# Sums of squares of the queries in a sliding-window attention layer: from small products on TensorE to transposes and sums on VectorE

## The chip, the cores and the metric

The kernel runs on one core of one Trainium2 chip. The metric is the device time of one execution in microseconds (us). Three runs of the kernel before took 1942.86, 1943.02 and 1943.11 us, so the median is 1943.02 us.

## The reference, cut to what matters

The reference is a decoder trunk of two layers on 1024 tokens of width 1024, in float32. Layer 0 mixes tokens by a short gated convolution, layer 1 by attention, and each is followed by a SwiGLU channel mixer. The change lies in the attention layer. There each of the 16 query heads of 64 features is normalised by its own root mean square before the scores are taken:

```python
def rmsnorm(x, gain):
    r = lax.rsqrt(jnp.mean(x * x, axis=-1, keepdims=True) + EPS)
    return (x * r) * gain

q = qkv[..., :q_end].reshape(bsz, s, N_KV_HEADS, GROUP, HEAD_DIM)
q = rmsnorm(q, q_gain)           # k in the same way
scores = einsum('bnqkgd,bnskd->bnkgqs', qb, kw) * scale   # blocks of 128 queries, 256 keys
logits = concatenate([scores - slope * dist (masked), sink], -1)
p = softmax(logits)[..., :-1]
out = einsum('bnkgqs,bnskd->bnqkgd', p, vw) @ w_o
```

So for each token and each query head one number is needed: the sum of the squares of 64 features.

## The kernel before, in words

Activations lie with features on the 128 partitions and tokens along the free axis. Every float32 product is made of three products in a reduced float32 format: each operand is split into a high and a low part (`hi`, `lo`), and hi*hi, hi*lo and lo*hi are added in PSUM. The large matrix products of the channel mixers are cut by a seven-product scheme; none of that is touched.

In the attention layer the 16 query heads are 8 tiles of 128 features (two heads each), numbered `i`. `project_k`, `project_v` and the tile-0 projection come first. Then, from line 1952, everything on TensorE, ScalarE, VectorE and GpSimd is in an order written out by hand. The loop at line 1965 projects tile `i` (the generator `product`, lines 165 and 169) in eight steps of six matmuls of 512 columns; `step` (line 1873) interleaves each of these steps with one unit of attention, a unit being one query tile and one block of 128 tokens. Units run ten steps behind the projection. The letters of `ORDER = "SPTMEDkPHLVOPK"` give the order inside a step:

- S: scores of the unit on TensorE (lines 1725 and 1726) into the one buffer of PSUM bank P0. M: VectorE adds the distance bias and takes the maximum, reading P0 (line 1739). E: exponentials of the unit before, on ScalarE (line 1757).
- T: the exponentials of two units before are transposed on TensorE (line 1765) into bank P1 or P3. H and L: ScalarE and VectorE split them into high and low parts (lines 1772 and 1778). V: product with the values, of three units before (lines 1790 and 1791). O: ScalarE and VectorE keep the result (lines 1807 and 1808).
- P, three times: two projection matmuls each. D: division steps that fall due; they use GpSimd (line 1596), four transposes (line 1601) and VectorE (line 1835).
- k and K: what has been planned with `plan(d, f)`. A `d` of x.5 runs at the k of the step after x, a whole `d` at the K that ends step x, counting from 0 at the first step after the tile's projection.

`keep_q(i, acc)` (line 1636) plans the rest of a projected query tile. `acc` is a pair of PSUM banks out of four, which the tile after next will use again. ScalarE squares both halves (`squares`, line 1654) from PSUM into `side`. `stats_of` (line 1656) makes eight products on TensorE: a block of 128 squared features x 128 tokens is the stationary operand and a matrix of two columns of ones and zeros, `half`, the moving one, so each token gets two sums (line 1513). VectorE scales them and adds epsilon (`head_mean`, line 1520), ScalarE takes Ln and Exp (lines 1532 and 1537), VectorE refines (lines 1539 to 1546). ScalarE copies the projected tile to `raw` in the slot G7 (line 1644). GpSimd spreads the factors to 64 columns each (`wide_of`, line 1596), TensorE turns them back to the feature layout (`rows_of`, line 1601) and VectorE multiplies `raw` (line 1606). `part_hi` (ScalarE, line 1681) and `part_lo` (GpSimd, line 1687) split the result into the operands of the scores. After each of the steps 0, 2, 3 and 5 a quarter of the next weights is split on ScalarE (line 137) and GpSimd (line 140).

Each engine runs its instructions in the order written, so an instruction that waits holds up those behind it.

Of the kernel before, what the change touches and what calls it, by code (L numbers as in the profile page):

```python
# [13 lines left out]
ALU = mybir.AluOpType  # L14

P = 128
D = 1024
T = 1024
NK = D // P
NB = T // P  # L20
# [61 lines left out]
def trunk_kernel(ctx: ExitStack, tc: tile.TileContext, xT, small, w_in, w_out, w_qk, w_v, w_o, w_gu, w_dn, out):  # L82
# [3 lines left out]
    dve, act, pool, pe = nc.vector, nc.scalar, nc.gpsimd, nc.tensor  # L86
    uid = [0]

    def slot(tag, shape=(P, D), dtype=F32, bufs=1):
        uid[0] += 1  # L90
        return sb.tile(list(shape), dtype, tag=tag, name=f"{tag}_{uid[0]}", bufs=bufs)
# [4 lines left out]
    def bank(tag):  # L96
        uid[0] += 1
        return pm.tile([P, 512], F32, tag=tag, name=f"{tag}_{uid[0]}", bufs=4 if tag == "acc" else 1)

    def plain(ap):  # L100
        return ap.bitcast(F32)
# [681 lines left out]
    def sums_of(a11, a12, a21, a22, s2, s3, s1, s4):  # L783

        return [
            lambda: dve.tensor_tensor(s3, a11, a21, ALU.subtract),
            lambda: dve.tensor_tensor(s2, a22, s3, ALU.subtract),  # L787
            lambda: dve.tensor_tensor(s4, a12, s2, ALU.subtract),
            lambda: dve.tensor_tensor(s1, a21, a22, ALU.add),
        ]  # L790
# [707 lines left out]
    def attention_layer():  # L1498
# [11 lines left out]
        def head_stats(st, sq, b0, n):  # L1510
            for b in range(n):
                o = 2 * (b0 + b)
                pe.matmul(st[:, o : o + 2], sq[:, b * P : (b + 1) * P], half, start=True, stop=True)
# [1 line left out]

        def head_mean(st):
            m = slot("hr_m", (P, NB, 2), bufs=2)
            dve.scalar_tensor_tensor(  # L1520
                m,
                st[:, 0 : 2 * NB].rearrange("p (b h) -> p b h", h=2),
                1.0 / HD,
                eps_r.unsqueeze(2).to_broadcast([P, NB, 2]),
                ALU.mult,
                ALU.add,
            )
            return m

        def head_log(m):  # L1530
            y = slot("hr_y", (P, NB, 2), bufs=3)
            act.activation(y, m, AF.Ln)
            return y

        def head_guess(y, inv):

            act.activation(y, y, AF.Exp, scale=-0.5)
            t = slot("hr_t", (P, NB, 2), bufs=2)
            dve.tensor_tensor(t, y, y, ALU.mult)
            if inv is not None:  # L1540
                dve.tensor_tensor(y, y, inv.unsqueeze(1).to_broadcast([P, NB, 2]), ALU.mult)
            return t

        def head_newton(y, t, m):
            dve.scalar_tensor_tensor(t, t, -0.5, m, ALU.mult, ALU.mult)
            dve.scalar_tensor_tensor(y, t, 1.5, y, ALU.add, ALU.mult)

        def head_r(m):
            y = head_log(m)
            head_newton(y, head_guess(y, None), m)  # L1550
            return y
# [41 lines left out]
        def spread(eng, wide, y):  # L1593

            copy = act.copy if eng is act else eng.tensor_copy
            copy(wide.rearrange("p (b h d) -> p b h d", b=4, h=2), y.unsqueeze(3).to_broadcast([P, 4, 2, HD]))

        def turn_blocks(pb, wide):
            for b in range(4):
                t = slice(b * P, (b + 1) * P)  # L1600
                pe.transpose(pb[:, t], wide[:, t], ident)  # L1601

        def scale_rows(raw, wide, q, pb):
            turn_blocks(pb, wide)
            c = slice(q * 512, q * 512 + 512)
            dve.tensor_tensor(raw[:, c], raw[:, c], pb, ALU.mult)

        def keep_k(g, raw, y):
# [13 lines left out]
                dve.tensor_tensor(lo[rest, e, :], raw[rows, :], plain(hi[rows, e, :]), ALU.subtract)  # L1622
            kz[g] = (hi, lo)

        g2 = slot("G2")
        s_bufs = [slot("s0", (P, 2, 2 * P))]
        s_bufs += [g2[:, h * 512 : h * 512 + 512].rearrange("p (e c) -> p e c", e=2) for h in (0, 1)]
# [8 lines left out]
        def keep_q(i, acc):  # L1636

            t = {}

            def copy(h):  # L1640
                if h == 0:
                    t["raw"] = slot("G7") if i + 1 < NK else t["both"][:, 0, :]
                src, c = acc.parts[h]
                act.copy(t["raw"][:, c], src)

            def squares(h):
                if h == 0:
                    if i + 1 < NK:
                        side = slot(f"G{5 + i % 2}")
                    else:  # L1650
                        t["both"] = slot("XS5", (P, 2, D))
                        side = t["both"][:, 1, :]
                    t["side"] = [side[:, h * 512 : h * 512 + 512] for h in (0, 1)]
                act.activation(t["side"][h], acc.half(h), AF.Square)

            def stats_of():
                t["st"] = bank(pos["free"])
                for h in (0, 1):
                    head_stats(t["st"], t["side"][h], 4 * h, 4)

            def mean():
                t["m"] = head_mean(t["st"])
                t["y"] = head_log(t["m"])

            def guess():
                t["t"] = head_guess(t["y"], cst[:, C_INVS + 2 * i : C_INVS + 2 * i + 2])

            def newton():
                head_newton(t["y"], t["t"], t["m"])


            def halves(e):
                rows = [slice(0, HD), slice(HD, P)]
                return rows[e], rows[1 - e]

            def part_hi(h, e):
                rows, _ = halves(e)
                if h == 0 and e == 0:
                    Q[i] = [slot(f"G{3 + i % 2}", dtype=F32R), slot(f"G{5 + i % 2}", dtype=F32R)]
                c = slice(h * 512, h * 512 + 512)  # L1680
                act.copy(Q[i][e][rows, c], t["raw"][rows, c])

            def part_lo(h, e):
                rows, rest = halves(e)
                c = slice(h * 512, h * 512 + 512)
                q = Q[i][e]
                pool.tensor_tensor(q[rest, c], t["raw"][rows, c], plain(q)[rows, c], ALU.subtract)

            rows_of = lambda h: scale_rows(t["raw"], t["side"][h], h, bank(pos["free"]))
            wide_of = lambda h: spread(pool, t["side"][h], t["y"][:, 4 * h : 4 * h + 4, :])  # L1690

            first, rows = (1, (4.5, 5.5)) if i + 1 < NK else (0, (5.5, 6.5))
            for d, fs in (
                (first, [lambda: squares(0)]),
                (first + 0.5, [lambda: squares(1)]),
                (1.5 + first, [stats_of, mean]),
                (2 + first, [guess, newton]),
                (rows[0] - 1.5 if first else 0, [lambda: copy(0)]),
                (rows[0] - 1.5, [lambda: wide_of(0)]),
                (rows[0] - 0.5 if first else 1, [lambda: copy(1)]),  # L1700
                (rows[0] - 0.5, [lambda: wide_of(1)]),
                (rows[0], [lambda: rows_of(0)]),
                (rows[1], [lambda: rows_of(1)]),
                (rows[1], [lambda: part_hi(0, 0), lambda: part_hi(0, 1)]),
                (rows[1] + 0.5, [lambda: part_lo(0, 0)]),
                (rows[1] + 1, [lambda: part_lo(0, 1)]),
                (rows[1] + 1.5, [lambda: part_hi(1, 0), lambda: part_hi(1, 1), lambda: part_lo(1, 0)]),
                (rows[1] + 2.5, [lambda: part_lo(1, 1)]),
            ):
                for f in fs:  # L1710
                    plan(d, f)
# [145 lines left out]
        pos = {"n": -LAG, "step": 0, "free": "P1"}  # L1857
        agenda = {}

        def plan(d, f):  # L1860

            agenda.setdefault(pos["step"] + d, []).append(f)
# [55 lines left out]
        for q in range(2):  # L1918
            raw = slot("WR", bufs=2)
# [10 lines left out]
        k1 = project_k(1)  # L1930
        st = bank("acc")
        head_stats(st, k0[1], 0, NB)
        m0 = head_mean(st)
        y0 = head_r(m0)
        v_ps = project_v(0)
        keep_v(0, v_ps)
        keep_k(0, k0[0], y0)
        st = bank("acc")
        head_stats(st, k1[1], 0, NB)
        m1 = head_mean(st)  # L1940
        y1 = head_r(m1)
        v_ps = project_v(1)
        keep_v(1, v_ps)
# [2 lines left out]
        acc = Acc()  # L1946
# [4 lines left out]
        E = mybir.EngineType  # L1951
        with tc.manual_schedule(engines={E.PE, E.Activation, E.DVE, E.Pool}):
            keep_q(0, acc)
            w = load_w(w_qk[1], NK, dve, pool)

# [9 lines left out]
            for i in range(1, NK):  # L1965
                acc = Acc()
                work = product(acc, w, xs)
                for k in range(NK):
# [10 lines left out]
                    if k in (0, 2, 3, 5):  # L1979
                        j = 2 * (0, 2, 3, 5).index(k)  # L1980
# [7 lines left out]
            free = ["XS3", "XS4"]  # L1988
            first_w = {}
            for m in range(NK):  # L1990
                acc = Acc()
                work = product(acc, w, o_split, len(early))
                for k in range(len(early)):
# [5 lines left out]
                    if m == NK - 1 and k == 0:  # L1999
# [4 lines left out]
                        for t, tag in enumerate(("WH", "WL")):  # L2004
                            raw = slot("WR", (P, len(late) * P), bufs=2)
# [16 lines left out]
        for e in (0, 1):  # L2022
            wide, rows, scale = divisions[NK // 2 - 1, 1, e]
# [22 lines left out]

    conv_layer()
    attention_layer()


# [87 lines left out]
```

## Time and profile before

| | |
|---|---|
| Median of three runs | 1943.02 us |
| Profiled execution | 1943.28 us, of which the span is 1941.4 us |
| TensorE (PE) busy | 1935.1 us (100% of the span) |
| Weight load (PEld) busy | 1618.2 us (83%) |
| VectorE (DVE) busy | 1371.3 us (71%) |
| ScalarE (ACT) busy | 871.2 us (45%) |
| GpSimd (POOL) busy | 246.2 us (13%) |
| DMA | 311.79 MB, mean 161 GB/s |

Busy shares are means over the whole span. The query tiles are projected between about 1025 and 1205 us, and there the shares differ from these means, so they are read from the stretch itself. A matmul on TensorE overlaps the one before it, so its listed duration is longer than the time by which it delays the next one; the time that a group takes on TensorE is the distance between starts, which the chain of waits shows.

### The profile page before, as it was taken

Reading aid. Unit: us, or ns where it says so; the run is one execution under the profiler, and the core shown is the slowest. Engines: PE = TensorE matmul, PEld = TensorE weight load, DVE = VectorE, ACT = ScalarE, POOL = GpSimd, SP = SyncE. Lnnn points to the kernel's source line nnn. Section 1 sums busy time; section 2 is a strip of 40 time slices with the busy share of each in tenths; the row PEclk is TensorE's granted clock in tenths of the full one; section 3 lists DMA queues with packets and bytes.
Section 4 is the critical chain, followed back from the end, with each engine's and each line's share of the span. In section 5 each row is a group of like instructions: output and inputs, shape, how many; then the busy total and the mean of one; then the engine's idle time right before and its main releaser. Section 6 shows DMA issues by size and latency. Waiting matters only on the chain.

```text
span 1941.4 us, 25504 instructions
## 1 busy us (share of the span) xinstructions
PE 1935.1 (100%) x9153; PEld 1618.2 (83%) x9153; DVE 1371.3 (71%) x2432; ACT 871.2 (45%) x1702; POOL 246.2 (13%) x344
## 2 busy tenths in 40 slices
PE   9999999999999999999999999999999999999999
PEld 8888888888888888888898888888888888888887
DVE  8998767876777676765644777788677766775543
ACT  5543434523333335444435888656233333344441
POOL 0000011011111110000004445310111111110000
PEclk9999999999999999999999999999999999999999
DMA  8422185244555548976300000152455455487562
GB/s 318 165 98 87 65 299 189 83 157 175 182 203 179 171 162 286 328 266 205 114 23 23 23 12 18 37 192 61 162 195 181 173 199 179 133 282 275 194 231 100
DMA packets 143167, 311.79 MB, mean 161 GB/s; under 512 B 13888, under 2 KB 53952, under 8 KB 143040
## 3 DMA queue, kind: packets, MB, share of 16 engines
q1 hardware_dynamic: 118992, 225.71, 34.6%
q0 software_dynamic: 23904, 84.42, 11.9%
q8 instruction: 72, 1.18, 0.3%
q14 instruction: 55, 0.45, 0.1%
q10 hardware_dynamic: 144, 0.03, 0.0%
HBM read 219.40 MB, written 90.70 MB: 160 GB/s over the span
## 4 chain that ended last, share of the span: by engine, by line
PE 95%; DVE 2%; issue 1%; ACT 1%; DMA 0%; ACTq 0%; DVEq 0%
PE acc L904 15%; PE acc L905 15%; PE acc L907 15%; PE P L904 9%; PE P L905 9%; PE P L907 9%; PE acc L165 6%; PE acc L169 3%; PE acc L1034 2%; PE acc L1032 2%; PE acc L1033 2%; PE P L1765 1%; PE P L1601 1%; PE P L1725 1%; PE P L1726 1%
## 5 line engine op out<-in xcount | busy, mean ns | idle before, releaser
L904 PE MATMUL acc<-XS,G 128*128 128x512 f32 x894 | 348.2, 389 | 0.0
L907 PE MATMUL acc<-XS,G 128*128 128x512 f32 x894 | 347.8, 389 | 0.0
L905 PE MATMUL acc<-XS,G 128*128 128x512 f32 x894 | 347.8, 389 | 0.0
L907 PEld LDWEIGHTS acc<-XS,G 128*128 128x128 f32 x894 | 167.8, 188 | 34.9
L904 PEld LDWEIGHTS acc<-XS,G 128*128 128x128 f32 x894 | 167.8, 188 | 34.9
L905 PEld LDWEIGHTS acc<-XS,G 128*128 128x128 f32 x894 | 167.8, 188 | 34.7
L907 PE MATMUL P<-A,G 128*128 128x512 f32 x502 | 195.3, 389 | 0.0
L905 PE MATMUL P<-A,G 128*128 128x512 f32 x502 | 195.3, 389 | 0.0
L904 PE MATMUL P<-A,G 128*128 128x512 f32 x502 | 195.3, 389 | 0.0
L907 PE MATMUL acc<-A,G 128*128 128x512 f32 x410 | 159.5, 389 | 0.0
L904 PE MATMUL acc<-A,G 128*128 128x512 f32 x410 | 159.5, 389 | 0.0
L905 PE MATMUL acc<-A,G 128*128 128x512 f32 x410 | 159.5, 389 | 0.0
L844 DVE TENSOR_TENSOR G<-WL,G 128x512 fp32r<-128x512 f32 x168 | 114.9, 685 | 53.1 <-ACT G L843 53.1
L843 ACT CAST G<-WR 128x512 fp32r<-128x512 f32 (+1 forms) x198 | 119.7, 605 | 67.3 <-PE acc L907 29.3
L165 PE MATMUL acc<-XS,WH 128*128 128x512 f32 x480 | 146.3, 405 | 0.6 <-ACT WH L137 0.6
L844 DVE TENSOR_TENSOR G<-WR,G 128x512 fp32r<-128x512 f32 (+1 forms) x198 | 131.8, 666 | 10.8 <-ACT G L843 10.5
L843 ACT CAST G<-WH 128x512 fp32r<-128x512 f32 (+1 forms) x156 | 93.7, 601 | 82.2 <-PE acc L907 36.8
L1204 ACT ACTIVATE G<-G 128x512 f32<-128x512 f32 x88 | 55.8, 634 | 162.1 <-DVE G L1275 158.0
L843 ACT CAST G<-WL 128x512 fp32r<-128x512 f32 x168 | 103.5, 616 | 37.3 <-DVE WL L787 33.5
L904 PE MATMUL P<-XS,G 128*128 128x512 f32 x290 | 112.9, 389 | 0.1
L907 PE MATMUL P<-XS,G 128*128 128x512 f32 x290 | 112.8, 389 | 0.0
L905 PE MATMUL P<-XS,G 128*128 128x512 f32 x290 | 112.8, 389 | 0.0
(316 smaller groups left out, 3898.1 us busy)
## 6 DMA issues: line engine op xcount, KB each, us to landing
G<-h SPq DMA_DIRECT2D x70, 512.0 KB, 5.2
h<-X POOLq DMA_DIRECT2D x44, 512.0 KB, 5.5
X<-in_w_dn SPq DMA_DIRECT2D x80, 256.0 KB, 3.7
s<-X POOLq DMA_DIRECT2D x40, 512.0 KB, 4.7
WR<-in_w_gu SPq DMA_DIRECT2D x36, 512.0 KB, 6.0
WH<-in_w_gu SPq DMA_DIRECT2D x36, 512.0 KB, 6.4
h<-X POOLq DMA_DIRECT2D x66, 256.0 KB, 4.0
WR<-s SPq DMA_DIRECT2D x52, 256.0 KB, 3.4
```

The lines of the kernel that those rows point to most:

```text
L165: pe.matmul(ps.half(h), wh, xs[:, j, c], start=first and j == 0, stop=False)
L169: pe.matmul(ps.half(h), wl, xs[:, 0, c], start=False, stop=last)
L843: lambda: act.copy(out_hi, raw),
L844: lambda: lo_eng.tensor_tensor(out_lo, raw, plain(out_hi), ALU.subtract),
L904: pe.matmul(ps, w[:, 0, c], x[:, 0, :], start=start and e == 0, stop=False, skip_group_check=True)
L905: pe.matmul(ps, w[:, 0, c], x[:, 1, :], start=False, stop=False, skip_group_check=True)
L907: pe.matmul(ps, w[:, 1, c], x[:, 0, :], start=False, stop=last, skip_group_check=True)
L1032: pe.matmul(ps, hi[:, kc], xs[:, 0, c], start=k == 0, stop=False, skip_group_check=True)
L1033: pe.matmul(ps, hi[:, kc], xs[:, 1, c], start=False, stop=False, skip_group_check=True)
L1034: pe.matmul(ps, lo[:, kc], xs[:, 0, c], start=False, stop=k == n_op - 1, skip_group_check=True)
L1204: state["silu"] = act.activation(x, x, AF.Silu)
L1601: pe.transpose(pb[:, t], wide[:, t], ident)
```

## The change

`stats_of` goes, and with it the eight small products of each query tile. The copy of the projected tile to `raw` comes first, both halves of it in the steps 1 (steps 0 and 1 for the last tile). Then `turn_raw(h)` turns four 128x128 blocks of `raw` on TensorE into the half of the accumulator that has just been copied, which puts tokens on the partitions, and ScalarE squares that half into `side`. `sums_of(h)` adds the 64 squares of each head on VectorE (`tensor_reduce`, 512 columns to 8), into the tile that `head_mean` then scales in place. `raw` is one tile in G7 for all query tiles but the last, where before a new one was taken for each. `rows_of`, `part_hi` and `part_lo` are planned one step later, save for the last tile. For the keys nothing changes but how `head_mean` is given its output.

```diff
+        raw_q = slot("G7")
             def copy(h):
                 if h == 0:
-                    t["raw"] = slot("G7") if i + 1 < NK else t["both"][:, 0, :]
+                    t["raw"], t["side"] = raw_q, None
+                    if i + 1 == NK:
+                        both = slot("XS5", (P, 2, D))
+                        t["raw"], t["side"] = both[:, 0, :], both[:, 1, :]
                 src, c = acc.parts[h]
                 act.copy(t["raw"][:, c], src)
-            def squares(h):
+            def turn_raw(h):
...
+                turn_blocks(acc.half(h), t["raw"][:, h * 512 : h * 512 + 512])
                 act.activation(t["side"][h], acc.half(h), AF.Square)
-            def stats_of():
-                t["st"] = bank(pos["free"])
-                for h in (0, 1):
-                    head_stats(t["st"], t["side"][h], 4 * h, 4)
+            def sums_of(h):
+                dve.tensor_reduce(
+                    t["m"][:, 4 * h : 4 * h + 4, :],
+                    t["side"][h].rearrange("p (b h d) -> p b h d", b=4, h=2),
+                    mybir.AxisListType.X,
+                    ALU.add,
+                )
-            first, rows = (1, (4.5, 5.5)) if i + 1 < NK else (0, (5.5, 6.5))
+            d0, rows = 0.5 if i + 1 < NK else 0, (5.5, 6.5)
             for d, fs in (
-                (first, [lambda: squares(0)]),
-                (first + 0.5, [lambda: squares(1)]),
-                (1.5 + first, [stats_of, mean]),
-                (2 + first, [guess, newton]),
-                (rows[0] - 1.5 if first else 0, [lambda: copy(0)]),
+                (d0, [lambda: copy(0)]),
+                (d0 + 0.5, [lambda: copy(1)]),
+                (d0 + 1, [lambda: turn_raw(0)]),
+                (d0 + 1.5, [lambda: sums_of(0)]),
+                (d0 + 2, [lambda: turn_raw(1)]),
+                (d0 + 2.5, [lambda: sums_of(1), mean]),
+                (d0 + 3, [guess, newton]),
                 (rows[0] - 1.5, [lambda: wide_of(0)]),
-                (rows[0] - 0.5 if first else 1, [lambda: copy(1)]),
                 (rows[0] - 0.5, [lambda: wide_of(1)]),
                 (rows[0], [lambda: rows_of(0)]),
                 (rows[1], [lambda: rows_of(1)]),
                 (rows[1], [lambda: part_hi(0, 0), lambda: part_hi(0, 1)]),
                 (rows[1] + 0.5, [lambda: part_lo(0, 0)]),
                 (rows[1] + 1, [lambda: part_lo(0, 1)]),
                 (rows[1] + 1.5, [lambda: part_hi(1, 0), lambda: part_hi(1, 1), lambda: part_lo(1, 0)]),
                 (rows[1] + 2.5, [lambda: part_lo(1, 1)]),
```

## Rows read from the trace of the kernel before

**Rows 1.** The page: busy time of TensorE; shares of the chain that ended last.

```profile
PE 1935.1 (100%) x9153; PEld 1618.2 (83%) x9153; DVE 1371.3 (71%) x2432; ACT 871.2 (45%) x1702; POOL 246.2 (13%) x344
PE 95%; DVE 2%; issue 1%; ACT 1%; DMA 0%; ACTq 0%; DVEq 0%
```

**Rows 2.** Windows in the query tiles: PE, PEld, DVE, ACT, POOL busy, clock, DMA.

```profile
1090.00:1112.00 22.00, 22.00 (x153) 19.96 (x152) 17.40 (x49) 17.75 (x54) 10.50 (x14) 1.00 0.08 26
1156.00:1178.00 22.00, 22.00 (x151) 19.79 (x150) 17.03 (x52) 19.01 (x57) 13.68 (x14) 1.00 0.06 21
```

**Rows 3.** Waits of TensorE's weight loads, 1020 to 1215 us: total, times, longest.

```profile
PEld P L1725 <- DVE mx L1739: 1.4, 6, 0.3
PEld P L1790 <- DVE A L1808: 0.7, 2, 0.5
```

**Rows 4.** Chain of waits around one group of small products: start, length, what.

```profile
1092.72 0.44 PE P L1765 x4
1093.15 1.68 PE P L1513 x16
1094.84 0.57 PE acc L165 x2
```

**Rows 5.** Chain of waits around four transposes of line 1601.

```profile
1034.54 0.44 PE P L1601 x4
1034.97 0.47 PE acc L165 x2
```

**Rows 6.** Line 1513 on TensorE for the query tiles: count, duration min/median/max, first and last start.

```profile
L1513 PE MATMUL P<-cst,G x112: 165/251/251, 1029.8 to 1171.1; 128*128 128x2 f32 x112
L1513 PE MATMUL P<-cst,XS x16: 166/251/251, 1190.8 to 1192.4; 128*128 128x2 f32 x16
```

**Rows 7.** Line 1601 on TensorE for keys and queries, in the same columns.

```profile
L1601 PE MATMUL P<-cst,G x72: 270/272/273, 999.3 to 1180.0; 128*128 128x128 f32 x72
L1601 PE MATMUL P<-cst,XS x8: 271/272/302, 1203.1 to 1206.2; 128*128 128x128 f32 x8
```

**Rows 8.** ScalarE's squares and copies of query tiles, in the same columns.

```profile
L1654 ACT ACTIVATE G<-acc x14: 578/588/597, 1025.4 to 1166.9; 128x512 f32<-128x512 f32 x14
L1644 ACT COPY G<-acc x14: 567/576/591, 1032.3 to 1175.3; 128x512 f32<-128x512 f32 x14
```

**Rows 9.** Groups on VectorE, 810 to 1120 us: busy, mean ns | idle before.

```profile
L139 DVE CAST WH<-WR 128x1024 fp32r<-128x1024 f32 x2 | 1.4, 693 | 14.0 <-PE acc L165 14.0
L1391 DVE TENSOR_TENSOR s<-s,WL 128x512 f32<-128x512 f32 x12 | 8.2, 686 | 0.6 <-ACT WL L1383 0.5
```

**Rows 10.** Groups on GpSimd in the same stretch.

```profile
L1687 POOL TENSOR_TENSOR G<-G,G 64x512 fp32r<-64x512 f32 x16 | 20.6, 1288 | 7.0 <-ACT G L1681 6.2
L140 POOL TENSOR_TENSOR WL<-WR,WH 128x256 fp32r<-128x256 f32 x18 | 13.2, 738 | 56.2 <-ACT WH L137 55.8 <-POOL G L1687 0.2
```

**Rows 11.** Timeline of GpSimd at step 0 of tile 3.

```profile
1085.10 0.61 POOL L1596 COPY s<-den 128x512 f32<-128x512 f32 x1 [0.26 <-DVE den L1825]
```

**Rows 12.** Timeline of TensorE: first scores of steps 2, 3 and 4 of tile 3.

```profile
1088.39 0.28 PE L1725 MATMUL P<-A,G 128*128 128x256 f32 x1
...
1091.61 0.28 PE L1725 MATMUL P<-A,G 128*128 128x256 f32 x1
...
1096.17 0.28 PE L1725 MATMUL P<-A,G 128*128 128x256 f32 x1
```

**Rows 13.** Timeline of ScalarE in step 2 of tile 3: an exponential, a high part.

```profile
1089.01 0.50 ACT L1757 ACTIVATE s<-s,mx 128x256 f32<-128x256 f32 x1
...
1090.47 0.58 ACT L1772 CAST G<-P 128x512 fp32r<-128x512 f32 x1
```

**Rows 14.** Timeline of VectorE in steps 2 and 3 of tile 3: L, O and M.

```profile
1091.08 0.69 DVE L1778 TENSOR_TENSOR G<-P,G 128x512 fp32r<-128x512 f32 x1
1091.81 0.43 DVE L1808 TENSOR_TENSOR G<-P,G 64x256 f32<-64x256 f32 x1
1092.29 0.54 DVE L1739 CUSTOM_DVE_ANT_0 G<-P,cst 128x256 f32<-128x256 f32 x1
```

More of the change, by code (lines that the diff above doesn't have):

```diff
@@ L1513, in head_stats, with head_mean @@
                 pe.matmul(st[:, o : o + 2], sq[:, b * P : (b + 1) * P], half, start=True, stop=True)
-        def head_mean(st):
-            m = slot("hr_m", (P, NB, 2), bufs=2)
+        def head_mean(m, st):
             dve.scalar_tensor_tensor(
                 m,
-                st[:, 0 : 2 * NB].rearrange("p (b h) -> p b h", h=2),
+                st,
                 1.0 / HD,
@@ L1527, in head_mean @@
             )
-            return m
         def head_log(m):
@@ L1641, in copy @@
                 if h == 0:
-                    t["raw"] = slot("G7") if i + 1 < NK else t["both"][:, 0, :]
+                    t["raw"], t["side"] = raw_q, None
+                    if i + 1 == NK:
+                        both = slot("XS5", (P, 2, D))
+                        t["raw"], t["side"] = both[:, 0, :], both[:, 1, :]
                 src, c = acc.parts[h]
                 act.copy(t["raw"][:, c], src)
-            def squares(h):
+            def turn_raw(h):
                 if h == 0:
[L1648 to L1653, printed above, removed]
-                act.activation(t["side"][h], acc.half(h), AF.Square)
-            def stats_of():
-                t["st"] = bank(pos["free"])
-                for h in (0, 1):
-                    head_stats(t["st"], t["side"][h], 4 * h, 4)
+                    side = slot(f"G{5 + i % 2}") if t["side"] is None else t["side"]
+                    t["side"] = [side[:, j * 512 : j * 512 + 512] for j in (0, 1)]
+                    t["m"] = slot("hr_m", (P, NB, 2), bufs=2)
+                turn_blocks(acc.half(h), t["raw"][:, h * 512 : h * 512 + 512])
+                act.activation(t["side"][h], acc.half(h), AF.Square)
+            def sums_of(h):
[5 more added lines that the diff above has]
+                )
             def mean():
-                t["m"] = head_mean(t["st"])
+                head_mean(t["m"], t["m"])
                 t["y"] = head_log(t["m"])
@@ L1932, in attention_layer @@
         head_stats(st, k0[1], 0, NB)
-        m0 = head_mean(st)
+        m0 = slot("hr_m", (P, NB, 2), bufs=2)
+        head_mean(m0, st[:, 0 : 2 * NB].rearrange("p (b h) -> p b h", h=2))
         y0 = head_r(m0)
@@ L1939, in attention_layer @@
         head_stats(st, k1[1], 0, NB)
-        m1 = head_mean(st)
+        m1 = slot("hr_m", (P, NB, 2), bufs=2)
+        head_mean(m1, st[:, 0 : 2 * NB].rearrange("p (b h) -> p b h", h=2))
         y1 = head_r(m1)
```

## The prediction

> **What bounds the kernel now.** I read the page first. TensorE is busy for the whole span and holds 95% of the chain that ended last; no other engine has over 2% of it [rows 1]. So an instruction taken from TensorE's queue shortens the run by its own time, as long as nothing else becomes late. Then the windows, to see whether that also holds where the change is. It does: in the query tiles TensorE fills its 22 us at a granted clock of 1.00, which is its upper level, 2.4 GHz. But the others are far busier there than their means: VectorE 17.0 to 17.4 of 22 us, ScalarE 17.8 to 19.0, GpSimd 10.5 to 13.7 [rows 2]. ScalarE at 81 to 86% is the engine with least room. Then the waits of TensorE's weight loads: between 1020 and 1215 us they are a few tenths each, the largest group 1.4 us in six waits for the maxima, which free the one bank P0 [rows 3]. TensorE is fed, with little to spare. Last come the chain and the timelines, for the price of each group and for the distance between the engines.
>
> **What leaves TensorE.** Eight small products per tile are 16 records, since each product of two float32 operands shows as two: 112 + 16 = 128 in eight tiles [rows 6]. In the chain a group takes 1.68 us, and the pair of projection matmuls behind it 0.57 us [rows 4] where such a pair otherwise takes 0.47 [rows 5]. So one tile pays 1.68 + 0.10 = 1.78 us, eight tiles 14.24 us. All of it is on the path that sets the end.
>
> **What comes to TensorE.** Eight transposes per tile in two groups of four. Line 1601 does the same operation, on blocks of the same size and type, and each of its transposes is one record: the two key tiles and eight query tiles have 80 [rows 7], which is 10 times 8. Four take 0.44 us, and the pair behind them 0.47, so nothing is added behind [rows 5]. Eight cost 0.88 us a tile, 7.04 us in all. The new ones write into an accumulator bank in place of a P bank, which no row shows. If they needed two records each, they would cost what the small products did, 14.24 us, and the gain would be zero. If the bank made no difference, 7.04. I take 7.04, since the transposes of lines 1765 and 1601, into two kinds of use of P banks, take the same 0.44 [rows 4, 5]. Nothing suggests less than that. TensorE's balance is 7.04 - 14.24 = -7.20 us.
>
> **What comes to VectorE.** Sixteen sums of 512 columns. No row shows this operation. From below, a cast of 1024 columns takes 0.693 us, so half of it 0.35; from above, a two-input operation of 512 takes 0.686 [rows 9]. That is 5.6 to 11.0 us in all, 0.7 to 1.4 a tile, in a tile of some 24 us (1029.8 to 1171.1 us is six tiles [rows 6]). I take 0.6, nearer the row of 512, because that has the same number of columns to read. VectorE goes from 79% to some 84% of the stretch, and the sum itself lies beside TensorE's work. Its cost is only in what it holds up.
>
> The Trainium skill speaks against this step: VectorE: DVE Perf Modes, section "Rules for kernel authors", calls this reduction the slowest operation of the engine, always at one element a cycle, and advises to restructure around it. By that page's clock 512 columns are an estimated 0.53 us before overhead. The trace has no such instruction to agree or differ. At the cast's 0.35 the scores of the six tiles that lose anything below would come some 0.25 us earlier each, 1.5 us in all, and the time would be 1936.2; by the rule's 0.53 it is within half a microsecond of my sum.
>
> **What only moves.** ScalarE has the same squares and copies as before, 0.588 and 0.576 us each [rows 8], GpSimd the same splits. Their order and their waits change, and here lie the losses. No DMA is issued by a moved step, and the weight splits on ScalarE and GpSimd keep their places behind steps 0, 2, 3 and 5, with two steps to the next tile.
> - `copy(1)` runs at the end of step 1, right behind the last `part_lo` of the tile before, which has moved to the same place and reads the half of `raw` that the copy overwrites. ScalarE waits there for GpSimd. Queued behind it are the exponentials, the first square and the next high part; the values and transposes on TensorE need those.
> - The first square waits for `turn_raw(0)`, in front of the high part. The transposes it waits for stand right behind those the high part needs anyway: 0.44 us, plus the square.
> - `sums_of` waits for the square, and on VectorE stands in front of the maxima of the next step; scores two steps on wait for these.
> - `turn_raw(h)` waits for a copy that was issued a step or more earlier.
>
> **Tile 3, worked through**, in before's times, each step by its row. On GpSimd a division ends at 1085.10 + 0.61 = 1085.7 [rows 11]. Three `part_lo` of 1.29 and one weight split of 0.74 follow [rows 10]: 1085.7 + 3.87 + 0.74 = 1090.3. ScalarE, by adding its durations, is there at about 1089.8, so it waits 0.5 us. Then copy to 1090.9, two exponentials of 0.5 to 1091.9, square to 1092.5, high part 0.58 to 1093.05 [rows 8, 13]. VectorE: low part 0.69 to 1093.75, keeping 0.43 to 1094.2, sum 0.35 to 0.69 to 1094.55 or 1094.9, two maxima, of which P0 is needed some 1.0 us, to 1095.6 or 1095.9 [rows 9, 14]. TensorE begins step 3 at 1091.61 + 0.44 = 1092.05; that step took 4.56 us with the stats and takes 4.56 - 1.78 + 0.44 = 3.22 now, so the scores of step 4 are due at 1095.27 [rows 4, 5, 12]. They wait 0.3 to 0.6 us; I take 0.5. The second sum and the mean in step 3 come with the same slack and I count nothing more for them.
>
> In an even tile the division falls differently: GpSimd is later, by 1.05 us at the copy, but step 2 has 0.44 us more on TensorE and the first unit's exponentials are short. By the same addition the scores come 0 to 0.2 us late; I take 0.2. So: tiles 3 and 5, 0.5 each; tiles 2, 4 and 6, 0.2 each; tile 7, whose copy needs no G7 and so doesn't wait, 0.3 for its shorter distance from turn to square; tiles 0 and 1 nothing, since few or no units run then. Together 1.0 + 0.6 + 0.3 = 1.9 us. The cover is thin: where a tile has ScalarE late by another 0.5 us, nearly all of it arrives at TensorE.
>
> **The sum.** -14.24 + 7.04 + 1.9 = -5.3 us. The profiled execution took 1943.28 us, span 1941.4 and 1.9 around it, and the median of the runs is 1943.02, 0.26 less. 1943.28 - 5.3 = 1938.0 for a profiled one, and 1937.7 for the median.
>
> **The rivals.**
> - *Nothing waits.* If ScalarE reaches the copy later than GpSimd is done, and the maxima are in time, the whole 7.2 us stays: 1935.8. For it: my chain is late by half a microsecond at most. Against: the waits for the maxima exist already [rows 3] and the new order adds work in front of them.
> - *The queues eat it.* The squares, the copies and the two halves of `part_hi` now stand in five successive steps on an engine at 81 to 86%. If each of tiles 2 to 7 loses 0.55 to 1.2 us in place of my 0.3, 3.3 to 7.2 us are gone: 1939.1 to 1943.0. The same result follows if the transposes take two records: -0 + 1.9, 1944.9.
> - *Slower, by GpSimd in front of the copy.* In tiles 1 to 6 ScalarE stands at `copy(1)` until the last `part_lo` ends. If GpSimd is one `part_lo` and one weight split later than I added, 1.29 + 0.74 = 2.03 us [rows 10], and nothing absorbs it, six tiles lose 12.2 us: 1943.02 - 7.2 + 12.2 = 1948.0. It decides from 1.2 us a tile on (7.2 / 6). For it: in an even tile I find 1.05 us of wait already. Against: exponentials have about a microsecond before their transposes need them, and steps 4 to 6 have less on ScalarE than before, so a delay doesn't grow from tile to tile.
>
> **How the numbers follow.** What a measurement of this kernel can tell from no change is about 0.2%, 3.9 us, so faster means under 1939.1 and slower over 1946.9. The forecast, losses of 1 to 3.3 us, 1936.7 to 1939.1: 0.38. Nothing waits, 1934.8 to 1936.7 (its low end gives back 1 us of today's waits): 0.26. The queues eat it, 1939.1 to 1946.9, the two-record case included: 0.23. Slower through GpSimd, over 1946.9: 0.13. Faster is the first two, 0.64. The range from 1934.8 to 1943.6 leaves out the slower case and some 0.05 of the one before; it holds both ends of the sum's cost and all of the losses up to 7.8 us.
>
> **What would show it.** Line 1513 keeps only the keys' 32 records; 64 more transposes of line 1601 stand in the accumulator banks, 0.44 us a group in the chain. The sums appear on VectorE with 0.35 to 0.69 us. ScalarE shows waits at line 1644 for GpSimd's line 1687, of half a microsecond in odd tiles and one in even ones. TensorE's waits for the maxima, line 1725, grow by one to two microseconds in total. I am wrong if the transposes into the accumulator cost more than 0.44 a group, if line 1725 or 1765 waits over 3 us more, or if TensorE's waits don't grow at all and the gain is whole.

## The result: slower by 0.4%, and the profile after

The changed kernel takes 1951.22 us (median of six runs, 1950.13 to 1953.12) against 1943.01 for the kernel before. The ratio is 1.0043, 95% interval 1.003 to 1.0056. The profiled execution has a span of 1949.5 us, 8.1 more than before. The forecast was 1937.7 and faster; the range ended at 1943.6.

The page of the changed kernel, busy time of TensorE, answers to [rows 1]: its busy time has hardly moved, although it has 64 records fewer.

```profile
PE 1936.0 (99%) x9089; PEld 1611.1 (83%) x9089; DVE 1382.4 (71%) x2448; ACT 870.5 (45%) x1702; POOL 246.6 (13%) x344
```

The instructions are those that were foreseen. Line 1513 (count, duration min/median/max, first and last start) is left with the keys' 32 records, 64 transposes write accumulators, against [rows 6, 7], and the sum on VectorE takes 0.686 us:

```profile
L1513 PE MATMUL acc<-cst,G x32: 165/251/251, 986.2 to 1002.0; 128*128 128x2 f32 x32
L1599 PE MATMUL acc<-cst,G x56: 270/272/273, 1028.7 to 1176.9; 128*128 128x128 f32 x56
L1599 PE MATMUL acc<-cst,XS x8: 270/272/273, 1197.4 to 1199.6; 128*128 128x128 f32 x8
L1658 DVE TENSOR_REDUCE hr_m<-G x14: 671/686/687, 1029.9 to 1179.8; 128x8 f32<-128x512 f32 x14
```

The waits of TensorE's weight loads between 1020 and 1225 us (total, times, longest) answer to [rows 3]. There were about 3 us of them; now there are 19:

```profile
PEld P L1730 <- DVE mx L1744: 8.7, 13, 1.0
PEld P L1795 <- DVE G L1813: 4.2, 6, 2.2
PEld P L1730 <- issue: 1.7, 3, 0.6
PEld P L1599 <- DVE G L1783: 1.7, 4, 0.5
PEld P L1795 <- DVE A L1813: 1.4, 2, 0.7
```

Scores (L1730) wait for the maxima, values (L1795) for VectorE's keeping of the result (L1813), which stands behind the refinement and the low part, and the division's transposes (L1599) for a P bank that the low part (L1783) still reads. The windows [rows 2] had TensorE busy for all of 22.00 us. A stretch of the changed kernel that ends in its longest wait, in the same columns:

```profile
1134.00:1156.00 22.00, 19.40 (x124) 16.06 (x122) 16.29 (x43) 18.00 (x52) 12.01 (x15) 1.00 0.01 1
```

**A ledger of steps.** The length of a step is the distance between the first scores of two steps in TensorE's timeline [rows 12]. From each I take the same step of the kernel before and what the counted instructions change (+0.44 in step 2, -1.78 + 0.44 in step 3, -0.44 in step 5 and +0.44 in step 7, where `rows_of` moved). Where nothing waits, nothing should be left, and so it is: step 3 of tile 4 went from 4.56 to 3.22 us, a rest of 0.00. What is left over, tiles 2 to 6 added up, in us (the total has the steps 0, 1 and 7 too, some -0.8 in every kernel, where waits of before are gone). The kernels below the first line are those of the next section:

| kernel | median | step 2 | step 3 | step 4 | step 5 | step 6 | total |
|---|---|---|---|---|---|---|---|
| changed | 1951.2 | 1.5 | 2.3 | 1.6 | 5.6 | 2.1 | 12.3 |
| copy_later | 1948.6 | 1.6 | 0.0 | 1.4 | 5.7 | 0.4 | 8.3 |
| short_sums | 1947.4 | 1.5 | 0.6 | 0.8 | 5.1 | 0.5 | 7.7 |
| log_later | 1944.8 | 1.6 | 2.4 | 1.9 | 1.5 | 0.2 | 6.8 |
| copy_log | 1942.5 | 1.5 | 0.0 | 1.6 | 1.5 | 0.2 | 4.2 |
| split_later | 1948.5 | 1.6 | 2.3 | 1.4 | 4.0 | 0.4 | 9.0 |
| products_back | 1960.0 | 1.5 | 0.2 | 0.0 | 4.6 | 2.0 | 7.6 |
| respaced | 1939.5 | 1.6 | 0.0 | 0.0 | 0.7 | 0.1 | 1.6 |
| respaced2 | 1938.3 | 0.0 | 0.0 | -0.1 | 0.8 | 0.1 | 0.2 |
| r2_split5 | 1937.6 | 0.0 | 0.0 | -0.1 | 0.0 | 0.0 | -0.8 |

For the changed kernel the ledger closes: -7.2 for the instructions, +12.3 here, +1.2 in tiles 0 and 1, +1.5 in tile 7 and +0.3 behind it make +8.1, the difference of the spans. The ledger reads one profiled execution of each kernel, the median all of its runs. r2_split1 has no line, because its profiled execution took 3997 us, twice as long as its others.

**One chain, at its worst.** The timeline of the changed kernel in steps 4 and 5 of tile 5 (start, length, engine; in brackets the idle time before and what ended it):

```profile
1150.83 0.18 DVE L1519 SCALAR_TENSOR_TENSOR hr_m<-hr_m,eps_r 128x16 f32<-128x16 f32 x1
1151.04 0.22 ACT L1530 ACTIVATE hr_y<-hr_m 128x16 f32<-128x16 f32 x1 [1.75 <-DVE hr_m L1519]
1151.16 0.61 ACT L1915 CAST A<-G 128x512 fp32r<-128x512 f32 x1
1153.22 0.20 ACT L1535 ACTIVATE hr_y<-hr_y 128x16 f32<-128x16 f32 x1
1153.57 1.28 POOL L1916 TENSOR_TENSOR A<-G,A 128x512 fp32r<-128x512 f32 x1
1153.67 1.21 DVE L1539 TENSOR_TENSOR hr_y<-hr_y,cst 128x16 f32<-128x16 f32 x1
1155.09 0.42 DVE L1783 TENSOR_TENSOR G<-P,G 128x256 fp32r<-128x256 f32 x1
1155.54 0.43 DVE L1813 TENSOR_TENSOR G<-P,G 64x256 f32<-64x256 f32 x1
1156.02 0.39 PE L1795 MATMUL P<-G,A 128*128 128x256 f32 x1 [1.79 <-DVE G L1813]
```

ScalarE stands 1.75 us at the logarithm (L1530) until the second sum and the mean are through VectorE. In this tile the first part of a split of an attention output (L1915) follows. The exponentials behind it come late, then the exponential of the root (L1535), then VectorE's four small steps of the refinement, which stand in front of the low part (L1783). One of them takes 1.21 us in place of 0.18, beside GpSimd's part of that split (L1916). The values on TensorE wait for all of it. And TensorE's clock falls. Windows of 2 us around that place (busy times of PE, PEld, DVE, ACT, POOL, then the clock):

```profile
1154.00:1156.00 2.00, 0.23 (x1) 0.00 (x0) 1.90 (x5) 1.62 (x6) 1.61 (x3) 1.00 0.00 0
1156.00:1158.00 2.00, 1.89 (x9) 1.46 (x10) 1.97 (x6) 1.43 (x5) 1.09 (x2) 0.85 0.00 0
1158.00:1160.00 2.00, 2.00 (x10) 1.70 (x9) 1.26 (x6) 0.39 (x3) 0.52 (x2) 0.50 0.36 114
1160.00:1162.00 2.00, 2.00 (x11) 1.78 (x10) 1.29 (x2) 0.69 (x2) 0.14 (x1) 0.80 0.08 26
1162.00:1164.00 2.00, 2.00 (x16) 1.85 (x15) 1.44 (x5) 1.61 (x6) 0.25 (x1) 1.00 0.00 0
```

After 1.8 us almost without work the granted clock is 0.50, the lower level of 1.2 GHz, for some 2 to 4 us. Step 6 of that tile takes 4.93 us in place of 3.21, 1.7 us for the clock. Step 5 loses 2.4 us, where the same step of tile 3 loses 0.8. So what is peculiar to tile 5 is some 1.6 + 1.7 = 3.3 us of the 12.3.

In copy_later and short_sums the same wait is there, but in their profiled executions the granted clock stayed at 1.00. Their 0.4 and 0.5 us in step 6, against 2.1, are therefore the clock's doing and not that of the edits.

### The profile page after: what moved, and what is told of

It is laid out like the page before. It is cut to its first block, busy times and chain, and to the rows that moved or that the text cites. A ratio compares the mean times of both kernels' runs of the same rounds, so it can differ in the third digit from the quotient of the medians.

```text
span 1949.5 us, 25381 instructions
## 1 busy us (share of the span) xinstructions
PE 1936.0 (99%) x9089; PEld 1611.1 (83%) x9089; DVE 1382.4 (71%) x2448; ACT 870.5 (45%) x1702; POOL 246.6 (13%) x344
```

## The experiments

Two theories. A: the loss is ScalarE's order. It stands at instructions that wait (for GpSimd at the copy, for VectorE at the logarithm), and the urgent work of attention stands behind. B: the loss is VectorE's work, sixteen sums of 0.68 us in front of maxima and low parts.

**copy_later.** The second copy moves behind the exponentials of step 2 (tiles 0 to 6).

```diff
-                (d0 + 0.5, [lambda: copy(1)]),
+                (d0 + (1 if i + 1 < NK else 0.5), [lambda: copy(1)]),
```

> Only copy(1) of tiles 0 to 6 moves, half a step later, behind the exponentials of step 2. Theory A (ScalarE's queue: it stands at an instruction that waits, and the exponentials and high parts behind it reach TensorE late): ScalarE's 6.7 us of waits for GpSimd in the changed kernel fall under 2, the losses of steps 2 and 3 (0.4 and 0.5 us a tile) shrink, and the time falls by 2 to 5 us, to 1946 to 1949. Theory B (VectorE: sixteen sums of 0.68 us in front of the maxima and low parts): no change, 1951 within 1.

1948.62 us, ratio to before 1.0029 (1.0018 to 1.004), 2.6 less than the changed kernel. Step 3 loses 0.0 in place of 2.3; step 2 loses what it lost. ScalarE's waits at the copy for GpSimd, in the changed kernel and here:

```profile
ACT G L1646 <- POOL G L1691: 6.7, 6, 3.0
```

```profile
ACT G L1646 <- POOL G L1691: 3.0, 1, 3.0
```

The wait that is left is one, in tile 1 (the expectation had under 2 us), and not in the steady tiles; they lose nothing in step 3. So the copy and its wait in front of the exponentials made the maxima late in step 3, as theory A has it. It is a fifth of the loss. That step 2 would get better was wrong.

**short_sums.** The sums read 4 of 64 squares.

```diff
-                    t["side"][h].rearrange("p (b h d) -> p b h d", b=4, h=2),
+                    t["side"][h].rearrange("p (b h d) -> p b h d", b=4, h=2)[:, :, :, 0:4],
```

> The sums on VectorE read 4 of each head's 64 squares and leave out the other 60; all else is the changed kernel. Theory B: some 0.55 us x 16 = 9 us of VectorE leave the way of the maxima, TensorE's waits for the maxima (8.7 us) mostly go, and the time falls by 8 to 14 us, to 1937 to 1943. Theory A: only ScalarE's wait at the logarithm gets shorter, by the sum in front of it, and the time falls by 1 to 4 us, to 1947 to 1950.

1947.43 us, ratio 1.0021 (1.0012 to 1.0029), 3.8 less. The sums now take 0.19 us in place of 0.69:

```profile
L1658 DVE TENSOR_REDUCE hr_m<-G x14: 171/186/188, 1029.9 to 1174.9; 128x8 f32<-128x32 f32 x14
```

Even so the kernel is slower than before; theory B alone would have given 1943 or less. Of the loss of the changed kernel, half is left in step 4, a quarter in step 3 and nearly all in step 5. Since copy_later alone takes away the loss of step 3 and short_sums three quarters of it, that loss needs both: the late copy and the sum in front of the maxima. ScalarE's wait at the logarithm (12.8 us in the changed kernel) shrinks with the sum in front of it but stays:

```profile
ACT hr_y L1530 <- DVE hr_m L1519: 8.1, 8, 1.3
```

**log_later.** The logarithm goes behind the next exponentials, the refinement behind the high and low part. (`log` is taken out of `mean` for this; that part of the edit is left out here.)

```diff
                 (d0 + 2.5, [lambda: sums_of(1), mean]),
-                (d0 + 3, [guess, newton]),
+                (d0 + 3, [log]),
+                (d0 + 3.5, [guess, newton]),
```

> Only the logarithm (ScalarE) moves half a step later, behind the exponentials of step 4, and the guess and the refinement another half step, behind the high and low parts of step 4. Theory A: ScalarE's 12.8 us of waits at the logarithm go, with them the losses of steps 4 and 5 (0.3 and 0.7 us a tile, 4.2 us in tile 5 with the lower clock behind it), and the time falls by 5 to 9 us, to 1942 to 1946. Theory B: the sums still stand in front of the maxima, the time falls by 0 to 2 us, to 1949 to 1951.

1944.75 us, ratio 1.0008 (0.9999 to 1.0017), 6.5 less: the largest effect of one edit, as theory A expected. Step 5 falls from 5.6 to 1.5 us and step 6 from 2.1 to 0.2. More than half of this is tile 5 (5.6 to 2.2 us in all its steps), where the refinement no longer meets GpSimd's operation and the clock stays at 1.00. In tiles 2, 3, 4 and 6 step 5 loses 0.1 to 0.6 us each in place of 0.7 to 1.0. Step 4, which was expected to gain, doesn't: it loses by the sum in front of the maxima (short_sums takes half of it, and respaced, with the sum behind them, all). ScalarE's wait at the logarithm in the changed kernel and here:

```profile
ACT hr_y L1530 <- DVE hr_m L1519: 12.8, 8, 2.1
```

```profile
ACT hr_y L1530 <- DVE hr_m L1519: 3.2, 6, 0.9
```

**copy_log.** Both of these edits together.

> The edits of the later copy and of the later logarithm together. They have cost 2.6 us and 6.5 us by themselves. If they are two separate stretches of ScalarE's queue they add up: 1951.2 - 9.1 = 1942.1, between 1941 and 1943.5. If both only shorten one and the same delay, which the one hands to the other, the time stays at 1943.5 to 1945.

1942.51 us, ratio 0.9996 (0.9987 to 1.0004). 2.6 + 6.5 = 9.1 were expected, 8.7 came. The two waits are separate costs: in the ledger step 3 is as in the one and steps 5 and 6 as in the other.

**products_back.** Eight small products per tile again, in step 3 behind the second transposes, their result unused.

```diff
                 turn_blocks(acc.half(h), t["raw"][:, h * 512 : h * 512 + 512])
+                if h == 1:
+                    st = bank(pos["free"])
+                    for j in (0, 1):
+                        head_stats(st, t["raw"][:, j * 512 : j * 512 + 512], 4 * j, 4)
```

> The changed kernel with the eight small products of each tile put back in step 3, where they stood, behind the second group of transposes; they read raw, their result goes to the free P bank and is used by nothing. Theory A (the products were the time in which ScalarE could stand at the logarithm at no cost): TensorE's waits of steps 3 to 5 vanish behind the 14.2 us, those of step 2 stay, and the time rises by 1 to 6 us, to 1952 to 1957. If the waits come from too much work on VectorE or ScalarE and not from its place, or have nothing to do with the products, nearly all of the 14.2 us is added: 1963 to 1966.

1959.97 us, ratio 1.0085 (1.0071 to 1.0098): 8.75 more than the changed kernel, outside both expectations. Of the 14.2 us put in, 5.5 are hidden. The ledger says where: steps 3 and 4 lose 0.2 and 0.0 in place of 2.3 and 1.6 and step 5 4.6 in place of 5.6, while steps 2 and 6 lose what they did. So the products had been cover for the waits of their own step and the next, but hardly for the logarithm's delay that arrives in step 5. TensorE's waits for the maxima here, against 8.7 in the changed kernel:

```profile
PEld P L1734 <- DVE mx L1748: 2.6, 6, 1.0
```

**split_later.** The first split of an attention output two steps later, away from the refinement of tile 5.

```diff
-                    if i == 6 and k == 2:
+                    if i == 6 and k == 4:
```

> The changed kernel with the first split of an attention output (ScalarE and GpSimd, in the loop of tile 6) two steps later, so that GpSimd's part no longer runs beside VectorE's refinement of tile 5, one instruction of which took 1.21 us in place of 0.18 and was followed by TensorE's longest wait, 2.2 us, and by a granted clock of 0.50 to 0.85 for some 4 us. If that meeting is what makes tile 5 so much worse than the others, its loss falls from 5.9 us to the 2 us of the others: 1951.2 - 4 = 1947, 1946 to 1948.5, and the clock stays at 1.00. If the order of the steps alone makes it: 1950 to 1951.5.

1948.53 us, ratio 1.0028 (1.0017 to 1.0038), 2.7 less (the span of the profiled execution 3.2 less), at the upper end of what the meeting was expected to give. Tile 5 loses 2.2 in place of 5.6 us, like its neighbours, the clock stays at 1.00, and the stretched instruction is gone (duration min/median/max; in the changed kernel the maximum is 1205 ns):

```profile
L1539 DVE TENSOR_TENSOR hr_y<-hr_y,cst x8: 174/176/176, 1033.6 to 1201.6; 128x16 f32<-128x16 f32 x8
```

The edit moves ScalarE's part of the split too, and the run doesn't separate the two. The timeline of the changed kernel does in part: from the logarithm to L1535 tile 5 takes 2.18 us and tile 3 1.66, and from there to the end of the refinement 1.95 and 0.92. So about 0.5 us of the longer wait in tile 5 is ScalarE's part and 1.0 the long operation.

**respaced.** All steps of the change kept, each put where it should hold up nothing. (`square` and `log` become functions of their own for this; left out here.)

```diff
-                (d0 + 0.5, [lambda: copy(1)]),
-                (d0 + 1, [lambda: turn_raw(0)]),
-                (d0 + 1.5, [lambda: sums_of(0)]),
-                (d0 + 2, [lambda: turn_raw(1)]),
-                (d0 + 2.5, [lambda: sums_of(1), mean]),
-                (d0 + 3, [guess, newton]),
-                (rows[0] - 1.5, [lambda: wide_of(0)]),
+                (d0 + 1, [lambda: copy(1), lambda: turn_raw(0)]),
+                (d0 + 1.5, [lambda: square(0)]),
+                (d0 + 2, [lambda: turn_raw(1), lambda: sums_of(0)]),
+                (d0 + 2.5, [lambda: square(1)]),
+                (d0 + 3, [lambda: sums_of(1), mean]),
+                (d0 + 3.5, [log]),
+                (d0 + 4, [guess, newton]),
+                (rows[0] - 1, [lambda: wide_of(0)]),
```

> The steps of the changed kernel spread so that none stands in front of urgent work on its engine: second copy behind the exponentials of step 2, each square behind the high part and not in front of it, each sum behind the maxima, logarithm behind the exponentials and refinement behind the next maxima; nothing is left out. If the loss is order alone (theory A, and B as far as the sums only stand at the wrong place), TensorE's waits fall under 6 us of the 19, and the time is 1936 to 1941, under both kernels. If VectorE's or ScalarE's amount of work is the bound, it stays over 1945.

1939.47 us, ratio 0.9982 (0.9973 to 0.999): faster than both kernels. Steps 3 and 4 lose nothing, step 2 what it lost.

**respaced2.** The first copy behind the high part of step 1 as well: `(d0 + (0.5 if i + 1 < NK else 0), [lambda: copy(0)])`.

> The respaced kernel with the first copy half a step later as well, behind the high part of step 1 (tiles 0 to 6). What is left there of TensorE's losses is 0.32 to 0.46 us in step 2 of four tiles, where the division's transposes wait for the low part of step 1, which the copy holds up. If that is the cause, 1.5 us go: 1937.5 to 1938.5. If the two high parts of the tile before are enough to hold it up: no change, 1939.5.

1938.29 us, ratio 0.9974 (0.9965 to 0.9984). Step 2 loses 0.0 in place of 1.6: it was the first copy, in front of a high part, that kept a P bank from the division's transposes. TensorE's waits:

```profile
PEld P L1599 <- POOL WL L140: 1.3, 1, 1.3
PEld P L1735 <- DVE mx L1749: 0.8, 2, 0.5
PEld P L1800 <- DVE G L1818: 0.8, 1, 0.8
```

The windows of the same kernel, against [rows 2], show TensorE full beside a VectorE and a ScalarE that are busier than in the kernel before, up to 19.2 and 19.9 of 22 us. So the amount of their work was not the bound:

```profile
1090.00:1112.00 22.00, 22.00 (x150) 19.67 (x149) 19.17 (x56) 18.53 (x57) 10.47 (x14) 1.00 0.08 26
1156.00:1178.00 22.00, 22.00 (x150) 19.72 (x149) 18.58 (x55) 19.90 (x60) 14.83 (x16) 1.00 0.04 13
```

**r2_split1 and r2_split5.** respaced2 with the split of tile 6's loop at `k == 1` and at `k == 5` in place of 2.

> The second respaced kernel with the first split of an attention output one step earlier (step 1 of the loop of tile 6). In tile 5 the scaling of the means on VectorE, 16 columns, took 1.18 us there in place of 0.18, while a two-input operation of GpSimd of 1.29 us ran, and TensorE lost 0.86 us in that tile. If the two meeting makes it so long, the operation is back at 0.18 and 0.5 to 0.9 us go: 1937.4 to 1937.8. If something else in tile 5 makes it: no change, 1938.3 within 0.3. ScalarE's part of the split now stands in its fullest steps and may give back up to 0.5.

> The same split three steps later (step 5) instead. If the meeting makes it: VectorE's operation is back at 0.18 and tile 5 loses under 0.2 us, 1937.4 to 1937.8; GpSimd is then later with the next tile's low parts, which may give back up to 0.5 in tile 6. If something else in tile 5 makes it: 1938.3 within 0.3.

1937.64 us (ratio 0.997, 0.9959 to 0.9982) and 1937.57 (0.9969, 0.9957 to 0.9981). Both end where the meeting theory put them. In the profile of the second, tile 5 loses nothing and the scaling of the means takes 0.38 us at most in place of 1.18.

## Why the prediction was wrong

- **What leaves and comes on TensorE: right.** -1.78 and +0.88 us a tile, one record for each transpose into an accumulator, no price for the other bank. The step with nothing waiting changes by exactly -1.34.
- **The sum on VectorE:** 0.6 taken, 0.686 measured, at the upper bound [rows 9]. The rule that the prediction cites from the Trainium skill (VectorE: DVE Perf Modes, "Rules for kernel authors"), one element a cycle, agrees: sums of 512 and of 32 columns took 0.686 and 0.186 us (short_sums), 1.04 ns a column, which is the estimated 0.53 us for 512, and 0.15 us besides. That the sum is the slowest operation doesn't show here; the two-input row of 512 columns took as long.
- **The copy behind GpSimd: right in kind, near in sum, wrong between odd and even tiles.** Waits of 0.5 us in odd tiles and 1.05 in even ones were worked out. Measured were 1.2 in tiles 3 and 5 and 0.3 to 0.6 in tiles 2, 4 and 6; tiles 3 and 4:

```profile
1090.75 0.59 ACT L1646 COPY G<-acc 128x512 f32<-128x512 f32 x1 [1.17 <-POOL G L1691]
1116.91 0.59 ACT L1646 COPY G<-acc 128x512 f32<-128x512 f32 x1 [0.55 <-POOL G L1691]
```

  That the scores of step 4 come later in odd tiles holds all the same: 0.75 us each against the 0.5 taken, and 0.4, 0.0 and 0.4 in even ones against 0.2. For tiles 2 to 6 the prediction has 1.6 us in step 3, the ledger 2.3; that this is so near is partly luck, since the waits it was worked out from came the other way round.
- **The step that failed** is "The second sum and the mean in step 3 come with the same slack and I count nothing more for them." The logarithm on ScalarE waits for exactly these and holds the exponentials behind it, and the refinement holds the low part. Steps 4 to 6 lost 9.3 of the 12.3 us, where the prediction has zero: 1.6 in step 4 by the second sum in front of the maxima, the rest behind the logarithm and the refinement, 3.3 of it by the meeting in tile 5 (split_later). log_later, with that order alone changed, gave 6.5 back, tile 5 included. The prediction's own sign of being wrong came with it: the waits for the maxima grew from 1.4 to 8.7 us. The worked example stopped one step too early: it followed the first half to the scores of step 4 and took the second half as a repetition, but only the second half ends in the mean, the logarithm and the refinement.
- **A second hole:** the first copy now stands in front of the high part of step 1. The prediction counts the copies among what moves, yet follows only the second one. It cost 1.5 us in step 2 (respaced2).
- **What covered the old order.** In the kernel before ScalarE stood at the logarithm too; its waits in all, and the one of tile 3 before and after:

```profile
ACT hr_y L1532 <- DVE hr_m L1520: 18.2, 7, 5.1
1095.08 0.22 ACT L1532 ACTIVATE hr_y<-hr_m 128x16 f32<-128x16 f32 x1 [2.17 <-DVE hr_m L1520]
1098.24 0.22 ACT L1530 ACTIVATE hr_y<-hr_m 128x16 f32<-128x16 f32 x1 [2.02 <-DVE hr_m L1519]
```

  Of the 18.2 us, 8.0 are in tiles 0 and 1, where few units run; in tiles 2 to 6 it was 10.1 us before and is 9.4 now. So the wait has not grown, but it has lost what lay beside it: before, TensorE spent 1.68 us of it on the small products [rows 4]. The prediction doesn't mention this wait. products_back shows that the cover was real, 5.5 us in all, of which the ledger has 3.7 in steps 3 and 4 and 1.0 in step 5. It was not all: most of the delay in step 5 stays and comes from where the logarithm and the refinement now stand (log_later).
- **The clock and the meeting in tile 5**, some 3.3 us, were in no rival.
- **The rival on the other side** gave the sign, and 1948.0, but not the mechanism: GpSimd in front of the copy is worth 2.6 us in the medians and 2.3 in the ledger (copy_later). Without it the kernel is still slower. Nor was it enough to shorten VectorE's sums to a quarter. That this rival's time came nearest is luck.
- **The gain was there.** With the order mended the same instructions take 1937.6 us, 5.6 under the kernel before beside it, of the 7.2 that the sum has for TensorE. By the steps of r2_split5, 2.1 us are lost in tile 7 and behind it, among them the wait of 1.3 us for GpSimd, and 0.4 in tiles 0 and 1; 0.8 are won back in tiles 2 to 6. What would mend tile 7 was not tried.

## What to carry to other kernels

When work is taken from the bounding engine, list first the waits of other engines that lay beside it: they are free only as long as it runs. Follow every moved instruction, the last half too, to what stands behind it on its own engine; an instruction that waits belongs behind the urgent work of its step, and half a step decided 6.5 us here, more than half of it through one meeting of two engines that it moved apart. A ledger of step lengths, with the counted instructions taken off, shows at once which step an order costs.

## What the hardware showed

A small operation on VectorE (16 columns, two operands in SBUF) that began while GpSimd ran a two-input operation of 256 or 512 columns lasted until 0.03 us after GpSimd's end, in all kernels here; only those that began in GpSimd's last 0.06 us took no longer than their usual 0.16 to 0.18 us. In respaced2, GpSimd and VectorE:

```profile
1144.74 1.29 POOL L1921 TENSOR_TENSOR A<-G,A 128x512 fp32r<-128x512 f32 x1
1144.88 1.18 DVE L1519 SCALAR_TENSOR_TENSOR hr_m<-hr_m,eps_r 128x16 f32<-128x16 f32 x1
```

In the changed kernel it was another small operation, 1.21 us, and it too ended 0.03 us after GpSimd's. Sums of 32 columns in short_sums, with one operand, kept their 0.17 to 0.19 us beside GpSimd. Three runs that moved GpSimd's operation (split_later, r2_split1, r2_split5) took the time back. The Trainium skill, GPSIMD Engine Reference, section "Specifications", says that GpSimd shares its SBUF interfaces with VectorE and contends with its instructions of two SBUF inputs; these traces agree.

The granted clock fell to 0.50 after 1.8 us in which TensorE had nothing to do, and in products_back after 1.5 us. In the profiled executions of copy_later and short_sums, with the same 1.8 us, it stayed at 1.00. So it isn't the kernel alone that decides. Of the eleven executions of short_sums four have a mean granted clock of 1.000 and took 1945.9 to 1946.1 us; seven have 0.999 and took 1947.3 to 1948.5. The changed kernel, copy_later and products_back have executions of both kinds too, the other experiments, whose TensorE never stands longer than 0.95 us in the query tiles, only such with 1.000. What decides between the two kinds was not tried.
